# Out projection of a hybrid decoder layer: its sums kept in PSUM over all row blocks, parts of x made pair by pair, weight ring of the second gate in another place

## The chip, the cores and the metric

One Trainium2 chip, one of its cores. Five engines work side by side, each on its own list of instructions in order: TensorE (PE) multiplies into PSUM, VectorE (DVE) and ScalarE (ACT) work elementwise and can read PSUM, GpSimd (POOL) works elementwise on SBUF, and SyncE (SP) issues most of the DMAs. The metric is the device time of one launch in microseconds (us), lower is better. It is the median of several runs.

## The reference

One decoder layer on x of 1024 tokens by 1024 columns, float32: SwiGLU with 2816 hidden rows, layer norm, a token mixer of two branches, layer norm, a second SwiGLU, layer norm.

```python
def swiglu(x, w_gate, w_up, w_down):
    return (jax.nn.silu(x @ w_gate) * (x @ w_up)) @ w_down

# in token_mixer
    y_a = hm @ w_branch_a
...
    y_b = yr @ w_branch_b
    merged = jax.nn.sigmoid(gate_a) * y_a + jax.nn.sigmoid(gate_b) * y_b
    return merged @ w_out

# in reference
        x = layer_norm(ALPHA * x + 0.5 * swiglu(x, ffn1_w_gate[l], ffn1_w_up[l], ffn1_w_down[l]),
                       ln1_g[l], ln1_b[l])
        mix = token_mixer(x, w_in[l], m_conv_w[l], ...
        x = layer_norm(ALPHA * x + mix, ln2_g[l], ln2_b[l])
        x = layer_norm(ALPHA * x + 0.5 * swiglu(x, ffn2_w_gate[l], ffn2_w_up[l], ffn2_w_down[l]),
                       ln3_g[l], ln3_b[l])
```

## The kernel before

**Every product is three matmuls.** A float32 operand is split into a high part (`nc.scalar.copy` to a rounded type, on ACT) and a low part (the difference, on POOL or DVE); `mm3` adds high by high, high by low and low by high into one PSUM bank. `split` (L126) makes the two parts, L130 is the high one, L134 the low one.

**The stages in order.** Gate and up projection of the first SwiGLU (`gate_first`, `gate_rest`), its down projection (`down_all`), the token mixer (`middle`, phases B and C), phase D (rest of branch a, out projection, second layer norm, parts of x for the second gate), gate and up projection of the second SwiGLU (`gate_rest`), its down projection (`down_all`), the last layer norm.

**The gate** works on 7 combinations of blocks of x and of the weights instead of 8 blocks. For each pair of token tiles `put_sums` makes the 7 sums and differences of x on DVE, transposes each on PE (`put`, L212), and writes the high part (ACT, L215) and the low part (DVE, L216). For each of the 22 hidden blocks f, `weights` makes the 7 sums of the weights (DVE, L254) and their splits (ACT and POOL, 7 of each), into the ring `wr` of 14 buffers, which holds one f; `gate_up` runs 7 products of 12 matmuls in the banks g, b and c, with the additions between them (L275, L299, L303 on DVE; L287, L291, L298 on ACT), and stores h in eight DMAs of 64 KB. The first f is done in two halves of 256 columns: half A needs the token pairs 0 and 1 only. The stores of the last f are issued by ACT, all others by SP. In the first gate the ring lies in a pool of its own on the left side of the memory, in the second in the pool R2 on the right side, with the raw weights `rw` and the sums `tw`, and the second down projection goes on using it.

**The down projection** (`down_all`) goes through the tokens in groups of 3, 3 and 2 tiles. A group holds up to 6 PSUM banks over all 22 rows of weights; each row is loaded and split again for each group. At the end the banks are added to the residual (L379) and the layer norm of each tile is run inside the next group.

**Phase D** does what is left of branch a (10 of its 16 products of 24 matmuls; the other 6 run in phase C and go to memory), and the out projection of 384 matmuls. It takes the rows of w_out two at a time, and for each token tile adds the product of two rows to the residual y in SBUF (`down`, L404), which makes 64 such additions. The layer norm of a tile follows its last addition (L415 to L429), and when all 8 tiles are done, `put_sums` runs for the four pairs.

**What sets the order.** A scheduler puts the instructions of each engine in an order; buffers are rings, and whoever writes one waits for its last reader. All loads of SP stand in one queue.

Of the kernel before, what the change touches and what calls it, by code (L numbers as in the profile page):

```python
# [8 lines left out]
F32 = mybir.dt.float32  # L9
# [21 lines left out]
class Net:  # L31
# [16 lines left out]
    RING = {"rw": (8, F32), "tw": (6, F32), "wr": (14, F32R), "e": (14, F32)}  # L48
# [11 lines left out]
    def ring(self, tag, n=512):  # L60

        bufs, dt = self.RING[tag]
        return {"e": self.ep, "wr": self.wp}.get(tag, self.rp).tile([P, 512], dt, tag=tag, bufs=bufs, name=self.nm(tag))[:, :n]
# [154 lines left out]
    def put_sums(self, cmb, p, a1, a2, s1):  # L218

        tt_ = self.nc.vector.tensor_tensor  # L220
        self.put(cmb[0], p, a1[0], "a")
        tt_(s1, a2[0], a2[1], op=ALU.add)
        tt_(a2[0], a1[0], a2[0], op=ALU.subtract)
        self.put(cmb[1], p, a1[1], "c")
        tt_(a1[0], s1, a1[0], op=ALU.subtract)
        self.put(cmb[2], p, a1[0], "d")
        self.put(cmb[3], p, a2[0], "c")
        tt_(a1[1], a1[1], a1[0], op=ALU.subtract)
        self.put(cmb[4], p, s1, "a")
        self.put(cmb[5], p, a2[1], "c")  # L230
        self.put(cmb[6], p, a1[1], "d")
# [38 lines left out]
    def gate_up(self, cmb, f, ws, hD, c0=0, c1=512):  # L270
# [35 lines left out]
    def gate_first(self, pre, src, cmb, hD):  # L306

        nc = self.nc
        B = []

        def pair(p):
            a = [[self.ring("e") for _ in range(2)] for _ in range(2)]
# [5 lines left out]
            self.put_sums(cmb, p, *a, self.ring("tw"))  # L318

        pair(0)  # L320
# [6 lines left out]
        self.gate_rest(pre, cmb, hD, 1)  # L327

    def gate_rest(self, pre, cmb, hD, f0):
        for f in range(f0, NF):  # L330
            ws = self.weights(*(self.raws(pre, f, 0) + self.raws(pre, f, 1)))
            if f == 0:
                self.gate_up(cmb, f, ws, hD, 0, 256)
                self.gate_up(cmb, f, ws, hD, 256, 512)
            else:
                self.gate_up(cmb, f, ws, hD)

    def down_all(self, pre, src, hD, ln_cb, hook=None):

        nc = self.nc  # L340
        wd = self.I[f"{pre}_w_down"][0]
        y, late = [], []
# [3 lines left out]
        for tag, shape, bufs in (("lng", [P, D], 1), ("hr", [P, 384], 4), ("lnb", [P, D], 1)):  # L346
            self.s(tag, shape, bufs=bufs)
        for t0, n in ((0, 3), (3, 3), (6, 2)):
            acc = [[self.ps(tag) for _ in range(2)] for tag in "gbc"[:n]]
            for f in range(NF):  # L350
                hr = self.s("hr", [P, 384], bufs=4)[:, :n * P]
# [1005 lines left out]
```

## Time and profile before

| what | us |
|---|---|
| median of 3 runs | 3258.95 (3255.22 to 3263.72) |
| profiled execution | 3261.03 |
| span of the profiled execution | 3259.1 |
| first gate | 0 to 470 |
| first down projection | 475 to 720 |
| phases B and C | 720 to 2332 |
| phase D, up to the second gate's first matmul | 2332 to 2555 |
| second gate | 2555 to 2995 |
| second down projection and last layer norm | 3000 to 3259 |

The profile lists for each instruction when it began, how long it took and what released it. Instructions of one engine overlap a little, so that durations add up to more than busy time. A busy share is an average over stages with different limits; what matters is where PE stands still, and for whom.

### The profile page before, as it was taken

How to read it: one execution, taken by the hardware profiler on the slowest of the kernel's cores; microseconds unless marked ns; L12 is line 12 of the kernel's file. 1: busy time of each engine (PE TensorE's matmuls, PEld its weight loads, DVE VectorE, ACT ScalarE, POOL GpSimd, SP SyncE). 2: the span in 40 equal slices, each digit the busy share in tenths (PEclk: the TensorE clock that was granted, in tenths of full speed). 3: DMA queues.
4: the chain of work that ended last, by engine and by line, in shares of the span. 5: the costliest groups of instructions: out<-in, count | busy, mean ns of one | idle time of the engine just before them, and what ended most of it. 6: DMA issues, size and time to landing. Idle time of an engine off the chain costs nothing. (4 is left out here: it accounts for less than half of the span.)

```text
span 3259.1 us, 45659 instructions
## 1 busy us (share of the span) xinstructions
PE 3084.5 (95%) x15888; PEld 2500.5 (77%) x15888; DVE 1928.2 (59%) x4820; ACT 1085.7 (33%) x1796; POOL 757.2 (23%) x819
## 2 busy tenths in 40 slices
PE   6999999999899999999999999999998799999997
PEld 6888878877677777887877777777776688887886
DVE  6444434683657676757577766476559744443557
ACT  3333324453312232323222222376332333332444
POOL 3444420011212222222222122200000344442000
PEclk8999999999889999999999999999999899999999
DMA  4223236662222222222232323474562322223665
GB/s 120 81 81 88 85 94 225 201 218 71 64 52 76 71 76 65 74 69 69 63 74 67 78 80 88 145 240 146 175 211 86 101 84 82 83 78 116 206 206 183
DMA packets 492908, 364.37 MB, mean 112 GB/s; under 512 B 114141, under 2 KB 415879, under 8 KB 492679
## 3 DMA queue, kind: packets, MB, share of 16 engines
q1 hardware_dynamic: 483463, 347.84, 36.2%
q0 software_dynamic: 4608, 8.39, 1.0%
q10 hardware_dynamic: 4608, 5.24, 0.5%
q8 instruction: 125, 2.05, 0.3%
q14 instruction: 104, 0.85, 0.1%
HBM read 280.61 MB, written 80.74 MB: 111 GB/s over the span
## 5 line engine op out<-in xcount | busy, mean ns | idle before, releaser
L150 PE MATMUL psg<-xT,wf 128*128 128x512 f32 x2328 | 632.1, 407 | 0.7 <-ACT f L860 0.7
L150 PEld LDWEIGHTS psg<-xT,wf 128*128 128x128 f32 x2328 | 422.3, 190 | 75.6 <-ACT f L860 1.1
L130 ACT CAST wr<-rw 128x512 fp32r<-128x512 f32 x396 | 243.9, 621 | 454.6 <-PE psc L150 243.0
L150 PE MATMUL psa<-xT,w 128*128 128x512 f32 x1200 | 317.9, 407 | 8.0 <-DVE pj L496 5.0
L134 POOL TENSOR_TENSOR wr<-tw,wr 128x512 fp32r<-128x512 f32 x176 | 229.2, 1304 | 264.2 <-ACT wr L130 258.3
L134 DVE TENSOR_TENSOR wr<-rw,wr 128x512 fp32r<-128x512 f32 x264 | 182.9, 699 | 178.7 <-ACT wr L130 167.6
L134 POOL TENSOR_TENSOR wr<-rw,wr 128x512 fp32r<-128x512 f32 x132 | 173.7, 1316 | 493.9 <-ACT wr L130 493.8
L150 PEld LDWEIGHTS psa<-xT,w 128*128 128x128 f32 x1200 | 223.5, 192 | 59.9 <-DVE pj L496 9.8
L275 DVE TENSOR_TENSOR e<-psb,e 128x512 f32<-128x512 f32 (+1 forms) x138 | 92.2, 668 | 296.6 <-PE psb L150 296.6
L150 PE MATMUL psb<-xq,wr 128*128 128x512 f32 (+1 forms) x1104 | 260.7, 386 | 6.5 <-DVE e L275 4.8
L150 PE MATMUL psc<-xq,wr 128*128 128x512 f32 (+1 forms) x1104 | 259.1, 384 | 1.5 <-DVE e L275 1.5
L150 PEld LDWEIGHTS psb<-xq,wr 128*128 128x128 f32 x1104 | 204.7, 192 | 48.5 <-issue 3.0
L150 PEld LDWEIGHTS psc<-xq,wr 128*128 128x128 f32 x1104 | 202.8, 190 | 43.5 <-DVE e L275 1.7
L150 PE MATMUL psg<-wr,wr 128*128 128x512 f32 x792 | 211.8, 397 | 16.4 <-ACT wr L130 11.4
L130 ACT CAST wr<-tw 128x512 fp32r<-128x512 f32 x176 | 109.0, 621 | 313.3 <-PE psb L150 226.6
L150 PE MATMUL psb<-wr,wr 128*128 128x512 f32 x792 | 209.1, 394 | 0.0
L150 PEld LDWEIGHTS psg<-wr,wr 128*128 128x128 f32 x792 | 149.1, 190 | 53.4 <-ACT wr L130 12.7
L134 POOL TENSOR_TENSOR w<-raw,w 128x512 fp32r<-128x512 f32 (+1 forms) x51 | 65.3, 1294 | 491.9 <-ACT w L130 430.6
L150 PEld LDWEIGHTS psb<-wr,wr 128*128 128x128 f32 x792 | 150.4, 190 | 31.7
L134 POOL TENSOR_TENSOR wf<-rawf,wf 128x512 fp32r<-128x512 f32 x98 | 129.7, 1339 | 166.9 <-ACT wf L130 151.6
L774 POOL TENSOR_SCALAR S<-S,PC 128x128 f32<-128x128 f32 x120 | 80.2, 668 | 292.6 <-DVE S L776 181.4
L150 PE MATMUL psc<-wr,wr 128*128 128x512 f32 x528 | 134.2, 389 | 0.0
(365 smaller groups left out, 5352.3 us busy)
## 6 DMA issues: line engine op xcount, KB each, us to landing
rw<-in_ffn_w_down_dram SPq DMA_DIRECT2D x264, 256.0 KB
rawf<-in_w_in_dram SPq DMA_DIRECT2D x98, 256.0 KB
rw<-in_ffn_w_gate_dram SPq DMA_DIRECT2D x88, 256.0 KB
rw<-in_ffn_w_up_dram SPq DMA_DIRECT2D x88, 256.0 KB
h<-e SPq DMA_DIRECT2D x336, 64.0 KB
hr<-h SPq DMA_DIRECT2D x88, 192.0 KB
raw<-in_w_in_dram SPq DMA_DIRECT2D x50, 256.0 KB
qkD<-f SPq DMA_DIRECT2D x32, 256.0 KB
```

Of the source, the lines that this page charges most:

```text
L130: nc.scalar.copy(hi, src)
L134: eng.tensor_tensor(lo, src, hi.bitcast(F32), op=ALU.subtract)
L150: self.nc.tensor.matmul(out, a[u], b[v], start=first and i == 0, stop=last and i == 2, skip_group_check=more)
L275: add = lambda o, a, b: nc.vector.tensor_tensor(o, a[:, cs], b, op=ALU.add)
L774: nc.gpsimd.tensor_scalar(S1, S, pcn, None, op0=ALU.mult)
```

## The change

- `gate_first` loads x of the pairs 0 to 2 before any sum is made, then makes pair 0's sums, loads pair 3, makes pair 1's sums, half A, the sums of the pairs 2 and 3, half B.
- `gate_up` stores h in two DMAs of 256 KB for each f. `gate_rest` loads the first two rows of the following down projection ahead of its last block (`row_load`, `ahead`), into a ring `hr` of the pools R1 and R2.
- All 16 products of branch a go to memory (`mix`, `mgD` is now 1024 by 1024). The out projection is `down_all` with w_out as its weights and 8 rows. Its layer norm calls `put_sums` when a pair of tiles is done: pair 0's in group 2, pair 1's in group 3, the others behind it. w_out is now loaded and split three times, not twice.
- The ring `wr` of the second gate lies in a pool W2 of its own on the right side, below R2 and E2; the second down projection has its own ring.
- `put_sums` takes a list of banks; `held` has the meaning that `loaded` had.

```diff
+    def row_load(self, wd, hD, t0, n, f):
+
+        hr, raws = self.ring("hr", n * P), [self.ring("rw") for _ in range(2)]
+        self.nc.sync.dma_start(hr, hD[f * P:(f + 1) * P, t0 * P:(t0 + n) * P])
+        for c in range(2):
+            self.loaded = self.nc.sync.dma_start(raws[c], wd[f * P:(f + 1) * P, c * 512:(c + 1) * 512])
+        return hr, raws
...
         def store(e, t):
-            for p in range(c0 // P, c1 // P):
-                dma(hv[:, e, p], t[:, p * P - c0:(p + 1) * P - c0])
+            dma(hv[:, e, c0 // P:c1 // P], t.rearrange("r (p t) -> r p t", t=P))
...
+        pair = lambda p: self.put_sums(cmb, p, *A[p], self.ring("tw"))
+        for p in range(4):
+            if p == 3:
+                pair(0)
+            A.append([[self.ring("e") for _ in range(2)] for _ in range(2)])
             for e in range(2):
                 for c in range(2):
-                    nc.sync.dma_start(a[e][c], src[(2 * p + e) * P:(2 * p + e + 1) * P, c * 512:(c + 1) * 512])
+                    nc.sync.dma_start(A[p][e][c], src[(2 * p + e) * P:(2 * p + e + 1) * P, c * 512:(c + 1) * 512])
             if p < 2:
                 B.extend(self.raws(pre, 0, p))
...
             ws = self.weights(*(self.raws(pre, f, 0) + self.raws(pre, f, 1)))
+            if f == NF - 1:
+                ahead = [self.row_load(wd, hD, 0, 3, i) for i in range(2)]
...
-    def down_all(self, pre, src, hD, ln_cb, hook=None):
+    def down_all(self, wd, nf, src, hD, ln_cb, hook=None, ahead=()):
...
-                if f % 3 == 2 and late:
+                if (f % 3 == 2 if nf == NF else f % 2) and late:
                     late.pop(0)()
...
+    def mix(self, xT, js, halves=(0,)):
+
+        its = [self.branch_a(j, lambda sl, g, j=j: self.nc.sync.dma_start(self.mgD[j * P:(j + 1) * P, sl], g)) for j in js]
+        alts = ["", "f"] if len(js) == 2 else ["f" if js[0] % 2 else ""]
+        self.proj_many(xT, its, self.I["w_branch_a"][0], alts, halves=halves, ps="g", lo_eng="dve")
...
+        def done2(tt, y):
+            nc.sync.dma_start(x2D[row(tt), :], y[tt])
+            if tt % 2:
+                net.put_sums(cmb, tt // 2, *([t[:, c] for c in c2] for t in y[tt - 1:tt + 1]), net.ring("tw"), "ad")
...
+            with net.phase("O", UB=5, side="right"):
+                net.wp = net.sp
+                net.down_all(ins["w_out"][0], NK, x1D, net.mgD, fin2, lambda: gb2.extend(rows("ln2")))
+            with net.pool("E2", "right") as net.ep, net.pool("W2", "right") as net.wp:
+                ahead = net.gate_rest("ffn2", cmb, h2, 0)
...
+    with net.phase("D", VB=6):
+        net.mix(hmT, (6, 7))
+        for j in range(0, NK, 2):
+            net.mix(hmT, (j, j + 1), (1,))
```

SP's queue at the start of the program, before: the loads of x for pair 2 (`e_374` on) stand behind the weights of f=1 (`rw_606` to `rw_612`), of f=2 and the first stores of h.

```order
L241 DMA rw_762<-in_ffn_w_gate_dram 128x4x128
L241 DMA rw_764<-in_ffn_w_up_dram 128x4x128
L241 DMA rw_766<-in_ffn_w_gate_dram 128x4x128
L241 DMA rw_768<-in_ffn_w_up_dram 128x4x128
L284 DMA h_77<-e_270 128x128 x2
L315 DMA e_374<-in_x_dram 128x512
L284 DMA h_77<-e_272 128x128 x2
L315 DMA e_375<-in_x_dram 128x512
```

And now; `e_122` to `e_125` are pair 2, `e_184` to `e_187` pair 3, `rw_602` on the weights of f=1.

```order
L318 DMA e_122<-in_x_dram 128x512
L318 DMA e_123<-in_x_dram 128x512
L318 DMA e_124<-in_x_dram 128x512
L318 DMA e_125<-in_x_dram 128x512
L318 DMA e_184<-in_x_dram 128x512
L318 DMA e_185<-in_x_dram 128x512
L318 DMA e_186<-in_x_dram 128x512
L318 DMA e_187<-in_x_dram 128x512
L243 DMA rw_602<-in_ffn_w_gate_dram 128x4x128
```

The loads of x have moved ahead of the weights of f=1 and of every store.

PE's queue where phase C ends, before: `psg_20608` is a product of phase C, `psb_21497` the first one of phase D's half 1, `psg_21287` another of phase C.

```order
L150 MATMUL psg_20608<-xT_19892,wf_20598 128x512
L150 MATMUL psg_20608<-xT_19891,wf_20599 128x512
L150 MATMUL psg_20608<-xT_19891,wf_20598 128x512
L150 MATMUL psb_21497<-xT_21320,w_21477 128x512
L150 MATMUL psg_21287<-xT_19891,wf_21277 128x512
```

And now, in the same place: `psg_20475` is what `psg_20608` was, `psg_21154` what `psg_21287` was.

```order
L151 MATMUL psg_20475<-xT_19759,wf_20465 128x512
L151 MATMUL psg_20475<-xT_19758,wf_20466 128x512
L151 MATMUL psg_20475<-xT_19758,wf_20465 128x512
L151 MATMUL psg_20475<-xT_19759,wf_20465 128x512
L151 MATMUL psg_21154<-xT_19758,wf_21144 128x512
```

The matmul with `w_21477` no longer stands between the two.

DVE's queue in the out projection, before: additions to y, splits of rows of w_out (`u`), the first layer norm.

```order
L404 SCALAR_TENSOR_TENSOR y_21357<-y_21357,psc_21777 128x512
L404 SCALAR_TENSOR_TENSOR y_21358<-y_21358,psc_21785 128x512
L404 SCALAR_TENSOR_TENSOR y_21358<-y_21358,psc_21793 128x512
L1124 TENSOR_TENSOR v_22418<-psg_22393,v_22418 128x512
L134 TENSOR_TENSOR u_21804<-u_21801,u_21803 128x1024
L134 TENSOR_TENSOR u_21810<-u_21807,u_21809 128x1024
L404 SCALAR_TENSOR_TENSOR y_21355<-y_21355,psc_21817 128x512
L404 SCALAR_TENSOR_TENSOR y_21355<-y_21355,psc_21825 128x512
L415 BN_STATS lnst_21834<-y_21355 128x6 x2
```

And now, in group 2: L135 are splits of rows for the matmuls, L217 and L225 to L230 belong to the sums of pair 0, L404 is now a layer norm's multiplication.

```order
L217 TENSOR_TENSOR xT_21648<-psd_22145,xT_21647 128x4x128
L135 TENSOR_TENSOR wr_22264<-rw_22251,wr_22263 128x512
L404 TENSOR_TENSOR u_21834<-u_21834,lng_21754 128x1024
L225 TENSOR_TENSOR u_21832<-u_21830,u_21832 128x512
L135 TENSOR_TENSOR wr_22301<-hr_22294,wr_22300 128x384
L227 TENSOR_TENSOR u_21830<-tw_22135,u_21830 128x512
L135 TENSOR_TENSOR wr_22305<-rw_22295,wr_22304 128x512
L230 TENSOR_TENSOR u_21830<-u_21830 128x512
L217 TENSOR_TENSOR xT_21650<-psd_22160,xT_21649 128x4x128
```

The 64 additions are gone from this queue; layer norm and sums of x now stand between the splits that feed PE.

## Rows read from the trace of the kernel before

**Rows 1.** The page's first part: busy time of each engine, its share of the span, instructions.

```profile
PE 3084.5 (95%) x15888; PEld 2500.5 (77%) x15888; DVE 1928.2 (59%) x4820; ACT 1085.7 (33%) x1796; POOL 757.2 (23%) x819
```

**Rows 2.** Windows: the stretch in us and its length, then busy time (and instructions) of PE, of PE's weight loads, of DVE, ACT and POOL, then the granted clock as a share, the DMA share and GB/s.

```profile
20.00:40.00 20.00, 12.66 (x80) 11.71 (x78) 9.02 (x16) 6.83 (x12) 7.93 (x6) 0.83 0.28 78
40.00:60.00 20.00, 14.46 (x84) 12.49 (x85) 14.60 (x22) 8.22 (x15) 1.63 (x1) 0.74 0.35 107
480.00:720.00 240.00, 238.11 (x1059) 195.37 (x1059) 150.71 (x282) 113.45 (x206) 3.91 (x3) 0.99 0.68 219
2455.00:2555.00 100.00, 73.98 (x316) 55.26 (x316) 92.94 (x181) 35.06 (x50) 0.00 (x0) 0.85 0.32 107
```

**Rows 3.** Timeline of PE at the start: start, duration, engine, line, operation, tiles, shape, count, and in brackets the idle time before it and what ended it.

```profile
34.91 1.60 PE L150 MATMUL psc<-xq,wr 128*128 128x256 f32 x12
40.47 0.81 PE L212 MATMUL psa<-ident,e 128*128 128x128 f32 x4 [3.96 <-DMA e<-in_x_dram]
...
72.96 2.21 PE L150 MATMUL psb<-xq,wr 128*128 128x512 f32 x9
```

**Rows 4.** Timeline of SP's queue at the start: a load of pair 2 and the seven behind it.

```profile
37.38 0.38 SPq L315 DMA_DIRECT2D e<-in_x_dram  x1
...
38.81 3.32 SPq L315 DMA_DIRECT2D e<-in_x_dram  x7
```

**Rows 5.** Timeline of DVE at the start: a subtraction beside POOL, two writes of x back to back, the last write of x.

```profile
55.14 1.76 DVE L254 TENSOR_TENSOR tw<-rw,rw 128x512 f32<-128x512 f32 x1
...
57.43 0.68 DVE L216 TENSOR_TENSOR xq<-psa,xq 128x512 fp32r<-128x512 f32 x1
58.03 0.68 DVE L216 TENSOR_TENSOR xq<-psc,xq 128x512 fp32r<-128x512 f32 x1
...
61.63 0.69 DVE L216 TENSOR_TENSOR xq<-psd,xq 128x512 fp32r<-128x512 f32 x1
```

**Rows 6.** Timeline of all engines between the first gate and its down projection.

```profile
469.69 4.11 ACTq L284 DMA_DIRECT2D h<-e  x8
...
471.02 0.69 DVE L303 SCALAR_TENSOR_TENSOR e<-e,e 128x512 f32<-128x512 f32 x1
...
474.31 0.51 ACT L130 CAST wr<-hr 128x384 fp32r<-128x384 f32 x1 [5.38 <-DMA hr<-h]
...
475.39 3.23 PE L150 MATMUL psg<-wr,wr 128*128 128x512 f32 x6 [5.13 <-ACT wr L130]
```

**Rows 7.** The same place of the second SwiGLU, PE alone.

```profile
2999.69 3.23 PE L150 MATMUL psg<-wr,wr 128*128 128x512 f32 x6 [5.07 <-ACT wr L130]
```

**Rows 8.** Timeline of PE where phase C ends.

```profile
2332.60 0.84 PE L150 MATMUL psg<-xT,wf 128*128 128x512 f32 x3
2336.95 0.50 PE L150 MATMUL psb<-xT,w 128*128 128x512 f32 x1 [3.51 <-ACT w L130]
2337.29 7.26 PE L150 MATMUL psg<-xT,wf 128*128 128x512 f32 x24
```

**Rows 9.** Timeline of PE: the last matmuls of the out projection, the first of the second gate, and the first of its second block f.

```profile
2513.50 5.89 PE L150 MATMUL psc<-u,u 128*128 128x512 f32 x24
...
2555.20 5.47 PE L150 MATMUL psg<-xT,wr 128*128 128x256 f32 x24 [1.19 <-ACT wr L130]
...
2584.55 2.94 PE L150 MATMUL psg<-xT,wr 128*128 128x512 f32 x12
```

**Rows 10.** Groups of DVE's instructions from 2455 to 2555 us, by shape: count, busy time, mean ns of one, idle time before them. The first and the last of 25 rows, and some between.

```profile
L404 DVE SCALAR_TENSOR_TENSOR y<-y,psc 128x512 f32<-128x512 f32 x36 | 24.3, 677 | 4.4 <-PE psc L150 4.0
L429 DVE SCALAR_TENSOR_TENSOR y<-y,lnr,lnb 128x1024 f32<-128x1024 f32 x8 | 9.9, 1277 | 0.0
...
L420 DVE TENSOR_TENSOR y<-y,lng 128x1024 f32<-128x1024 f32 x7 | 8.5, 1215 | 0.0
L415 DVE BATCH_NORM_STATS2 lnst<-y 128x6 f32<-128x512 f32 x12 | 8.0, 683 | 0.0
...
L164 DVE SCALAR_TENSOR_TENSOR lnr<-rst,lnr 128x2 f32<-128x2 f32 x12 | 1.8, 149 | 0.1
...
L425 DVE TENSOR_SCALAR lnv<-lnmv 128x2 f32<-128x2 f32 x4 | 0.6, 158 | 0.0
```

**Rows 11.** Groups of DVE's instructions in the first down projection, 480 to 720 us: the splits.

```profile
L134 DVE TENSOR_TENSOR wr<-rw,wr 128x512 fp32r<-128x512 f32 x123 | 84.1, 689 | 85.8 <-ACT wr L130 78.8 <-PE psc L150 5.4 <-issue 0.3
L134 DVE TENSOR_TENSOR wr<-hr,wr 128x384 fp32r<-128x384 f32 x41 | 22.6, 551 | 0.0
```

**Rows 12.** Windows of 100 us in the first gate and in the second, columns as in Rows 2.

```profile
200.00:300.00 100.00, 100.00 (x443) 82.81 (x442) 43.49 (x61) 31.68 (x53) 47.24 (x38) 1.00 0.28 79
...
2700.00:2800.00 100.00, 100.00 (x432) 81.07 (x431) 41.96 (x58) 30.84 (x52) 46.19 (x37) 1.00 0.28 80
```

**Rows 13.** Timeline of PE in the first gate and in the second, each with two groups of 12 matmuls that follow each other.

```profile
249.77 2.88 PE L150 MATMUL psb<-xq,wr 128*128 128x512 f32 x12
252.49 2.88 PE L150 MATMUL psc<-xq,wr 128*128 128x512 f32 x12
...
2930.32 2.96 PE L150 MATMUL psb<-xq,wr 128*128 128x512 f32 x12
2933.11 2.95 PE L150 MATMUL psc<-xq,wr 128*128 128x512 f32 x12
```

More of the change, by code (lines that the diff above doesn't have):

```diff
@@ L336, in gate_rest @@
                 self.gate_up(cmb, f, ws, hD)
[L338 removed]
+        return ahead
+    def row_load(self, wd, hD, t0, n, f):
[5 more added lines that the diff above has]
+    def down_all(self, wd, nf, src, hD, ln_cb, hook=None, ahead=()):
         nc = self.nc
[L341 to L342 removed]
+        y, late, ahead = [], [], list(ahead)
         if self.wp is self.sp:
             self.ring("wr")
[L346 to L347 removed]
         for t0, n in ((0, 3), (3, 3), (6, 2)):
             acc = [[self.ps(tag) for _ in range(2)] for tag in "gbc"[:n]]
[L350 to L352 removed]
+            for f in range(nf):
+                hr, raws = ahead.pop(0) if ahead else self.row_load(wd, hD, t0, n, f)
+                if (t0, f) == (6, 17):
+                    self.held = self.loaded
                 h = self.ring("wr", n * P), self.ring("wr", n * P)
@@ L1226, in build @@
                 net.wp = net.sp
-                net.down_all("ffn1", x, h1, fin1, hook1)
+                net.down_all(ins["ffn1_w_down"][0], NF, x, h1, fin1, hook1, ahead)
         middle(net, ins, x1T, x1D)
-        y, gb2 = [], []
-        def load_ln():
-            gb2.extend((net.bcast_row(ins["ln2_g"], "lng"), net.bcast_row(ins["ln2_b"], "lnb")))
-        def load_y(hh):
-            for tt in range(4 * hh, 4 * hh + 4):
-                nc.sync.dma_start(y[tt], x1D[row(tt), :])
-        def fin2(tt):
-            net.layer_norm(tt, y, *gb2, lambda t: nc.sync.dma_start(x2D[row(t), :], y[t]))
@@ L1243, in build, with rows @@
-        c2 = slice(0, 512), slice(512, 1024)
-        with net.phase("D", UB=10, VB=5, side="right"):
-            load_ln()
-            v = [net.half() for _ in range(5)]
-            yt = [net.s("y", [P, D], bufs=8) for _ in range(8)]
-            y.extend(yt[4:] + yt[:4])
-            net.mix_out(net.hmT, y, fin2, load_y)
-            a, b = net.new_xT(), net.new_xT()
-            gw.close()
+        gw.close()
+        gb2, gb3 = [], []
+        c2 = slice(0, 512), slice(512, 1024)
+        def rows(v):
+            return net.bcast_row(ins[v + "_g"], "lng"), net.bcast_row(ins[v + "_b"], "lnb")
@@ L1252, in build, with fin2 @@
+        def fin2(tt, y):
+            net.layer_norm(tt, y, *gb2, lambda t: done2(t, y))
+        def done2(tt, y):
+            nc.sync.dma_start(x2D[row(tt), :], y[tt])
+            if tt % 2:
+                net.put_sums(cmb, tt // 2, *([t[:, c] for c in c2] for t in y[tt - 1:tt + 1]), net.ring("tw"), "ad")
+        with net.rings("R2"):
             xp = xs.enter_context(net.pool("X2"))
-            (a11, a12), (s2, s3), (s1, a22) = net.halves(a), net.halves(b), net.halves([net.big(xp) for _ in range(2)])
+            (a11, a12), (s2, s3) = (net.halves(net.new_xT()) for _ in range(2))
+            s1, a22 = net.halves([net.big(xp) for _ in range(2)])
@@ L1254, in build @@
             d = net.big(xp)
             cmb = [a11, a12, s2, s3, s1, a22, (d[:, 0:4], d[:, 4:8])]
-            for p in range(4):
-                net.put_sums(cmb, p, *([y[2 * p + e][:, c] for c in c2] for e in range(2)), net.half())
-        with net.rings("R2"):
-            net.wp = net.rp
-            with net.pool("E2", "right") as net.ep:
-                net.gate_rest("ffn2", cmb, h2, 0)
+            with net.phase("O", UB=5, side="right"):
+                net.wp = net.sp
+                net.down_all(ins["w_out"][0], NK, x1D, net.mgD, fin2, lambda: gb2.extend(rows("ln2")))
@@ L1273, in middle @@
     with net.phase("B", VB=4):
-        with tc.issue_after(net.loaded.ins):
+        with tc.issue_after(net.held.ins):
             net.rwkv_small(x1T)
@@ L1311, in middle @@
             net.mlstm_chunk(c)
-        hmT = net.hmT = [net.new_xT()]
+        hmT = [net.new_xT()]
         with net.low():
```

113 lines of the change are left out of this document (27 added, 86 removed).

## The prediction, made before the changed kernel ran

> **What bounds the kernel now.** I read the page first: PE is busy for 95% of the span, DVE for 59% [rows 1]. So a gain must come from places where PE stands still, or from a stage where its matmuls follow each other more slowly than elsewhere. The windows find the places: 20 to 60 us has PE at 27.1 of 40 us with a clock of 0.74 to 0.83, and 2455 to 2555 has it at 74.0 of 100, while DVE there is busy for 92.9 [rows 2]. The timeline adds two stops of 5.1 us, between each gate and its down projection [rows 6, 7]. Elsewhere there is little to take: in the first down projection PE works 238.1 of 240 us [rows 2]. The windows of the two gates show the slower stage: 443 matmuls in 100 us in the first, 432 in the second, both at a clock of 1.00 and with the other engines alike [rows 12].
>
> In phases B and C the instructions of PE stand in the same order as before, so I count nothing there.
>
> **The start.** Half A ends at 34.91 + 1.60 = 36.5 us. Then PE waits 4.0 us for x [rows 3], because the loads of pairs 2 and 3 are issued from 37.38 to 42.1 us, behind weights and stores [rows 4]. The last part of x is written by DVE at 61.63 [rows 5], and the next f's matmuls run evenly from 72.96 on [rows 3], 11.3 us later. Now x is there early. What is left behind half A is 13 writes of x and 4 other steps of DVE; back to back one takes 0.60 us (57.43 to 58.03 [rows 5]), so 17 x 0.60 = 10.2, with 1.0 for the first transposition and cast. Ten subtractions move into half A, beside POOL's work; such a one took 1.76 us instead of 0.69 [rows 5], and half A's own additions stand behind them in DVE's queue. That is 10 x 1.07 = 10.7 us at most, nothing if they fit in DVE's idle time there (11 of 20 us, [rows 2]); I take 3, as POOL's seven splits cover only a part of half A. So: 36.5 + 3 + 11.2 + 11.3 = 62.0 instead of 73.0, **-11 us**. Bounds: -14 with no delay; -4 with the whole of it.
>
> **Gate to down projection, twice.** ACT issues the eight stores of the last f in 4.11 us, 0.51 each, and the casts for the first matmul stand behind them: the cast at 474.31, the matmul at 475.39 [rows 6]. Now there are two issues; the second one waits for DVE's last step, which ends at 471.71 [rows 6]. 471.7 + 0.5 + 1.1 (cast to matmul, as now) = 473.3, **-2.1** each, -4.2 together. The rows of weights were not what it waited for, so their earlier loads count nothing. Bounds: 0 to -5 each, as the slow first matmuls behind a stop (six take 3.23 us [rows 6], where 6 x 0.227 = 1.4) may go too. A page of the Trainium skill speaks against this term: "DMA: Bandwidth & Descriptors", in its section on the fixed cost, puts a sequencer's dispatch of a DMA at about 50 ns. By it eight issues are 0.4 us and this term would be -0.3; the row has 4.11, so I keep the row's.
>
> **End of phase C and branch a.** PE stops for 3.51 us at 2333 for a matmul of phase D whose weights were cast late, and the 24 matmuls behind it, which could have run, take 7.26 us instead of 24 x 0.227 = 5.4 [rows 8, 13]. That matmul has left its place, so both go. From 2332.6 on 284 matmuls are left of branch a: 284 x 0.227 = 64.4, with 2 us for four places where PE now waits until DVE has read its bank (each at most the 0.69 us of that step, less the matmuls that stand between; 5.4 in all if the old stop stays in some form): 2399. Then a new wait: the first cast of the out projection stands behind the last addition of branch a, as it overwrites its buffers: two steps of 0.69 and two casts of 0.5 to 0.6, with their hand-overs 2.8 us: 2401.8. The transfers of this stretch, 1.28 MB for each 24 matmuls or 5.44 us, make 235 GB/s; in the first down projection 219 GB/s went beside PE at 238.1 of 240 us [rows 2], so I count them as hidden.
>
> **Out projection.** The same 384 matmuls. Group 1 holds 8 rows of 18: 144 x 0.227 = 32.6, with 1.5 for the first splits: 2435.9. From there DVE decides, and its work is counted from rows [rows 10, 11]: 15 rows of splits (0.551 + 2 x 0.689) = 28.9; 16 additions out of PSUM at 0.68 = 10.9; 8 layer norms (2 x 0.683, 1.215, 1.277 and two small steps, 4.2) = 33.6; 4 inverse roots (11 steps of 0.15) = 6.6; 28 writes of x and 16 sums at 0.683 = 30.1; 6 sums of weights at 0.69 = 4.1. Together 114. Durations overlap: in the window from 2455 to 2555 the 25 rows add up to 105 us and DVE is busy for 92.9 [rows 2, 10], so 114 x 0.885 = 101. It stood idle for 7.1 of those 100 us; now two group ends wait for PE, so I take 10, and 1 to the first matmul: 2435.9 + 101 + 10 + 1 = 2548, before 2555.2 [rows 9]. **-7**. What cost 64 additions now costs 16, but a third of the splits is new, and all the layer norms and sums remain on DVE; that is why the gain is small. The stretch from the gate's first matmul to its even pace (29.4 us, to 2584.55) I leave as it is: PE gets the last transpositions first, as before. Bounds: -15 with DVE never idle and both stops at 2333 and 2399 gone; +10 if DVE stands idle for 27 instead of 10 us.
>
> **The second gate's pace.** 12 matmuls take 2.79 us there and 2.72 in the first gate [rows 13]; the seven products of a block f make 0.49 us, 22 blocks (less the first, in halves) 21 x 0.49 = 10.3. The order of work is the same in both gates; what differs is where the operands lie: in the first gate the ring of the weights lies below x, in the second at the upper end of the memory, far above x. The down projections have both operands in one ring, the first at 0.225 a matmul (238.1 over 1059 [rows 2], smaller ones among them), so it is only this combination that is slow. The ring now lies next to x's parts, below the rings it was above. No row shows this new place; the bounds are 0 and -10.3, and I take **-10.3**, since all stretches but that one run at 0.227. A rule of the Trainium skill says the opposite: "SBUF — State Buffer", section "Who interferes with whom", gives PE read ports of its own and lets only the port that DVE and GpSimd share contend. By it the place of a ring changes nothing and this term is 0, which is the first rival; the row of 2.79 it doesn't explain.
>
> **Sum.** -11 - 4.2 - 7 - 10.3 = -32.5 against the profiled execution's own time, 3261.03 (span 3259.1 and 1.9 around it): 3228.5. That execution is 2.1 above the median of 3258.95; against the median it is 3226.5. I say 3228.
>
> **The rivals.**
> 1. *The pace stays.* The second gate goes on at 2.79, whatever the reason for it is. Against it: nothing but the place differs. For it: no row shows the new place. -22: 3239.
> 2. *The out projection gives nothing, and the pace stays.* DVE, busy for 93% of the window now, stays the bound; each idle piece that the new order brings costs in full, and the time saved at 2333 goes into it. With D at 0 and the start at -6: -10, 3250, the same.
> 3. *Slower: DVE and PE wait for each other in the groups 2 and 3.* The writes of x for pairs 0 and 1 (14 of them) now stand in DVE's queue between the splits, and their transpositions in PE's queue behind matmuls that need such splits. Before, no matmuls stood ahead of them there. If each write waits for a whole row of PE (18 or 12 matmuls, 4.1 or 2.7 us, 3.4 in the middle), that is 14 x 3.4 = 48 us: 3228.5 + 48 = 3276. It decides for slower from 3.0 us for each write on (14 x 3.0 = 42, the 32.5 gained and 9.8). Against it: the ring holds two rows ahead, and the first down projection runs layer norms with transpositions between its splits while PE works 238.1 of 240 us [rows 2].
> 4. *The change doesn't reach the start:* x is early, but half A gets longer by as much, since POOL and DVE slow each other. Start 0, rest as forecast: 3239.
>
> **How the numbers follow.** Forecast 0.42; rivals 1 and 4 together 0.27; rival 2 0.17; rival 3 0.08; still more gain (no idle time on DVE, half A not delayed, both down projections at -5, about 3212) 0.06. About 0.3% (9.8 us) is what a measurement of this kernel can tell from no change. Faster: 0.42 + 0.27 + 0.06 = 0.75, of which I give 0.02 to the same; the same 0.17 + 0.02 = 0.19; slower 0.08. The range leaves out rival 3 and most of the far gain: from 3213 to 3256, the upper end 3 us short of the old median for rival 2 with the start at its worst.
>
> **What would show it.** Start: no wait for x at 40 us, and even groups of 12 matmuls from about 62 us on. Gates' ends: stops of 3.1 us instead of 5.1. Phase C's end: no stop for weights at 2333 (the times shifted by the start's gain). Out projection: DVE above 90% from the end of group 1 to the second gate, waits of PE for splits in group 3; PE waiting in pieces of 3 us or more in group 2 means rival 3. Second gate: 443 matmuls in 100 us, or 432 for rival 1. The forecast is wrong as a whole if phases B and C, which nothing touches, come out longer by themselves.

## The result, and the profile after

The changed kernel took 3242.07 us (median of 4 runs, 3237.07 to 3244.4), the one before on the same chip 3259.64: a ratio of 0.993, with a 95% interval of 0.9911 to 0.9949. On another chip it was 3240.21 beside 3266.22, 0.9917 (0.9899 to 0.9934). So the change saves 18 to 26 us, clear of no change but less than the 31 forecast: 3228 was forecast, with a range of 3213 to 3256.

The page's first part after: DVE has 20 us less to do than in [rows 1], PE 7, and the span is 18.8 shorter.

```profile
PE 3077.5 (95%) x15888; PEld 2496.7 (77%) x15888; DVE 1908.0 (59%) x4812; ACT 1097.3 (34%) x1836; POOL 757.8 (23%) x819
```

**Start.** Windows, columns as in [rows 2]:

```profile
20.00:40.00 20.00, 15.04 (x105) 13.68 (x105) 17.60 (x26) 8.39 (x16) 9.61 (x6) 0.91 0.29 81
40.00:60.00 20.00, 18.01 (x136) 16.16 (x135) 16.14 (x25) 10.63 (x20) 8.74 (x6) 1.00 0.22 64
```

PE's timeline after, with the place where [rows 3] had a wait of 3.96 us for x:

```profile
35.47 1.67 PE L151 MATMUL psb<-xq,wr 128*128 128x256 f32 x12 [1.73 <-DVE e L277]
37.19 1.66 PE L151 MATMUL psc<-xq,wr 128*128 128x256 f32 x12
38.69 0.60 PE L213 MATMUL psc<-ident,e 128*128 128x128 f32 x4
...
60.55 2.88 PE L151 MATMUL psb<-xq,wr 128*128 128x512 f32 x12
```

Half A ends at 38.85 (37.19, with 1.66), 2.3 us later than the 36.5 of before, since DVE has the first pairs' subtractions ahead of its additions. In exchange the parts of x follow at once, and the even pace begins at 60.55 instead of 72.96.

**First gate to first down projection.** All engines, to be held against [rows 6]:

```profile
457.26 2.57 ACTq L285 DMA_DIRECT2D h<-e  x2
...
458.59 0.69 DVE L304 SCALAR_TENSOR_TENSOR e<-e,e 128x512 f32<-128x512 f32 x1
459.88 0.51 ACT L131 CAST wr<-hr 128x384 fp32r<-128x384 f32 x1 [3.37 <-DVE e L304]
...
460.96 3.23 PE L151 MATMUL psg<-wr,wr 128*128 128x512 f32 x6 [3.13 <-ACT wr L131]
```

The stop is 3.13 us instead of 5.13. The cast now begins 0.05 us after ACT has issued the two stores (457.26 + 2.57 = 459.83). Before, it began 0.5 us after the end of the eight issues, and what released it was the load of the first row of h [rows 6], which the change has moved ahead as well. The six slow matmuls behind the stop are unchanged.

**End of phase C to the second gate.** PE's timeline of the mix (what is left of branch a's products) and the first matmul of the out projection (before: [rows 8, 9]):

```profile
2341.46 5.70 PE L151 MATMUL psg<-xT,wf 128*128 128x512 f32 x24 [0.88 <-DVE h L1108]
2350.89 7.32 PE L151 MATMUL psg<-xT,w 128*128 128x512 f32 x24 [3.73 <-DVE v L1108]
...
2398.91 0.55 PE L151 MATMUL psg<-wr,wr 128*128 128x512 f32 x1 [2.63 <-ACT wr L131]
```

The stop of 3.51 us at 2333 is gone. In its place stands one of 3.73, with slow matmuls behind it (24 in 7.32). The wait before the out projection, 2.63, is the one foreseen (2.8). Then windows of group 2, of group 3, and of the pairs' end up to the gate's first matmul:

```profile
2434.00:2473.00 39.00, 39.00 (x187) 32.22 (x186) 37.77 (x75) 20.98 (x37) 0.00 (x0) 1.00 0.61 198
2473.00:2502.00 29.00, 24.21 (x110) 16.87 (x108) 28.77 (x71) 14.49 (x26) 0.00 (x0) 1.00 0.60 191
2502.00:2535.00 33.00, 13.90 (x57) 9.80 (x57) 29.03 (x54) 11.02 (x18) 0.07 (x1) 0.55 0.19 72
```

DVE is busy for 95.6 of 101 us, above the 90% that the forecast named; PE works all through group 2 and stands idle for 19 us of the last 33.

**The second gate's pace** is still 432 in 100 us, as in [rows 12] (PE alone: instructions, clock, DMA share, GB/s):

```profile
2600.00:2700.00 100.00, 100.00 (x432) 1.00 0.29 83
```

**Second gate to second down projection.** Where [rows 7] had one stop of 5.07, there are now two:

```profile
2971.14 2.63 ACTq L285 DMA_DIRECT2D h<-e  x2
...
2974.95 0.50 PE L151 MATMUL psg<-wr,wr 128*128 128x512 f32 x1 [3.19 <-ACT wr L131]
...
2979.05 0.56 DVE L135 TENSOR_TENSOR wr<-hr,wr 128x384 fp32r<-128x384 f32 x1 [5.83 <-DMA h<-e]
...
2980.26 2.50 PE L151 MATMUL psg<-wr,wr 128*128 128x512 f32 x5 [4.81 <-DVE wr L135]
```

The first is the short one that was forecast. The second is new: DVE's split waits 5.83 us for the last stores of h, although it reads nothing of them. It writes a buffer of the new ring, and that lies where the last store reads its e tile: in the program as built the buffer begins at byte 167360 of a partition, the e tile at 167872, and each is 2048 long.

Set side by side, the same matmuls of two executions give a ledger: how much each stretch adds to the time after against before, in us (minus is a gain). The second pair of profiles is from the repeats told below.

| term | forecast | first pair | second pair |
|---|---|---|---|
| start, to the first gate's even pace | -11 | -12.4 | -13.9 |
| first gate to first down | -2.1 | -1.8 | -3.0 |
| phases A to C | 0 | +6.2 | -2.3 |
| end of C to the second gate's even pace | -7 | -14.8 | -16.5 |
| the second gate's pace | -10.3 | 0.0 | 0.0 |
| second gate to the end | -2.1 | +4.0 | +3.1 |
| span | -32.5 | -18.8 | -32.6 |

Three rows differ from the forecast by more than 5 us in both pairs, and one only in the first.

### The profile page after: what moved, and what is told of

Same layout as the page of the kernel before. It is cut to its first block, busy times and chain, and to the rows that moved or that the text cites. A ratio compares the mean times of both kernels' runs of the same rounds, so it can differ in the third digit from the quotient of the medians.

```text
span 3240.3 us, 45588 instructions
## 1 busy us (share of the span) xinstructions
PE 3077.5 (95%) x15888; PEld 2496.7 (77%) x15888; DVE 1908.0 (59%) x4812; ACT 1097.3 (34%) x1836; POOL 757.8 (23%) x819
## 5 line engine op out<-in xcount | busy, mean ns | idle before, releaser
L151 PE MATMUL psg<-xT,wf 128*128 128x512 f32 x2352 | 640.6, 409 | 1.6 <-DVE h L1108 0.9
L151 PEld LDWEIGHTS psg<-xT,wf 128*128 128x128 f32 x2352 | 429.0, 191 | 78.2 <-ACT wf L131 1.3
L131 ACT CAST wr<-rw 128x512 fp32r<-128x512 f32 x444 | 273.2, 621 | 490.5 <-PE psc L151 276.7
L135 DVE TENSOR_TENSOR wr<-rw,wr 128x512 fp32r<-128x512 f32 x312 | 215.5, 697 | 197.2 <-ACT wr L131 186.5
L135 POOL TENSOR_TENSOR wr<-tw,wr 128x512 fp32r<-128x512 f32 x176 | 229.9, 1308 | 248.9 <-ACT wr L131 234.9
L135 POOL TENSOR_TENSOR wr<-rw,wr 128x512 fp32r<-128x512 f32 x132 | 173.4, 1314 | 481.9 <-ACT wr L131 481.7
L151 PE MATMUL psg<-wr,wr 128*128 128x512 f32 x936 | 253.4, 398 | 23.5 <-DVE wr L135 13.3
L151 PE MATMUL psb<-wr,wr 128*128 128x512 f32 x936 | 250.5, 395 | 0.0
L151 PEld LDWEIGHTS psg<-wr,wr 128*128 128x128 f32 x936 | 175.8, 190 | 69.0 <-DVE wr L135 20.7
L151 PEld LDWEIGHTS psb<-wr,wr 128*128 128x128 f32 x936 | 178.1, 191 | 37.3
L135 POOL TENSOR_TENSOR w<-raw,w 128x512 fp32r<-128x512 f32 (+1 forms) x51 | 65.5, 1297 | 491.5 <-ACT w L131 429.9
L135 POOL TENSOR_TENSOR wf<-rawf,wf 128x512 fp32r<-128x512 f32 x98 | 130.0, 1342 | 169.6 <-ACT wf L131 154.0
L151 PE MATMUL psc<-wr,wr 128*128 128x512 f32 x624 | 160.1, 391 | 0.0
```

Source lines behind the costliest of these rows:

```text
L131: nc.scalar.copy(hi, src)
L135: eng.tensor_tensor(lo, src, hi.bitcast(F32), op=ALU.subtract)
L151: self.nc.tensor.matmul(out, a[u], b[v], start=first and i == 0, stop=last and i == 2, skip_group_check=more)
```

## Experiments

Each kernel is the changed one with the edit shown. Where an expectation says "12.4 us earlier" or the like, it is a row of this ledger. The medians of one kernel differ by some us from measurement to measurement (the kernel before 3259.64 to 3266.22, the changed one 3242.07 and 3240.21), so what an edit of 10 us is worth is read from the same matmuls in its trace and in the changed kernel's.

**128 bytes between the second gate's pools**

```diff
-            with net.pool("E2", "right") as net.ep, net.pool("W2", "right") as net.wp:
+            with net.pool("E2", "right") as net.ep, net.pool("pad2", "right") as pp, net.pool("W2", "right") as net.wp:
+                pp.tile([P, 32], F32, tag="pad2", bufs=1, name="pad2")
```

> The changed kernel with 128 more bytes between the second gate's pools, so that its weight ring begins at 137024 bytes of a partition instead of 137152; nothing else moves. Theory A (the address): a matmul goes at 227 ns when its weights and its columns begin at the same offset of 256 bytes, and at 232 when the two offsets differ by 128, as they do in the second gate before and after the change (weights at 192 of 256, x at 64) and in no other place. Then the second gate goes at 2.72 us per 12 matmuls, PE is busy with 443 instead of 432 instructions in 100 us, and the time falls by 10.3 us, to about 3232. Rival B (the place: which end of the partition the ring lies at, or what else runs then): the pace stays at 2.79 and the time at 3242, within 3.

3232.52 us. The gate runs at 443:

```profile
2700.00:2800.00 100.00, 100.00 (x443) 1.00 0.29 83
```

From its even pace to its end the same matmuls gain 10.0 us on the changed kernel. The place of the ring is that of the changed kernel but for 128 bytes, so the place is not the reason: theory A holds. (An offset is meant here as the address in a partition, modulo 256 bytes.)

**The mirror: 128 bytes in the first gate**

```diff
-            with net.pool("W1") as net.wp, net.pool("X1") as xp, net.pool("E1", "right") as net.ep:
+            with net.pool("W1") as net.wp, net.pool("pad1") as pp, net.pool("X1") as xp, net.pool("E1", "right") as net.ep:
+                pp.tile([P, 32], F32, tag="pad1", bufs=1, name="pad1")
```

> The changed kernel with 128 bytes put between the first gate's weight ring and its x, so that x there begins at 192 of 256 and the weights still at 64; the ring stays where it was. Theory A (offsets that differ by 128 cost 5.8 ns a matmul): the first gate, 21 row blocks of 84 matmuls, falls from 443 to 432 instructions in 100 us and the time grows by 10.2 us, to about 3252. Rival B (the place of the ring or what else runs decides): the first gate keeps 443 and the time stays at 3242, within 3.

3252.1 us, 10.0 above the changed kernel's 3242.07, and 9.9 more in the first gate by the same matmuls, which goes at the second's pace:

```profile
200.00:300.00 100.00, 100.00 (x432) 1.00 0.30 85
```

A ring below x, fast until now, becomes slow by 128 bytes. Both directions are shown. The pads leave one rival, that each operand has to begin at 64 of 256, whatever the other does. The second down projection of the changed kernel speaks against it: weights and columns lie in one ring there, both at 192 in the program as built, and they go at the fast pace.

```profile
3060.00:3160.00 100.00, 100.00 (x443) 1.00 0.60 194
```

**64 bytes in the second gate.** The edit of the first experiment with a tile of [P, 16].

> The changed kernel with 64 more bytes between the second gate's pools: the weight ring begins at 128 of 256 bytes, x at 64. Theory A (128 bytes' difference alone costs, through which of two halves of 256 bytes an operand begins in): 64 and 128 lie in different halves, so the pace stays at 2.79 us per 12 matmuls and the time at 3242. Theory B (any difference of the offsets costs): the same. Theory C (only a difference of just 128 costs, 64 doesn't): 443 instructions in 100 us and -10.3 us, about 3232. So a fast pace leaves C alone, a slow one A or B.

The pace stays slow, so theory C falls:

```profile
2600.00:2700.00 100.00, 100.00 (x430) 1.00 0.30 87
```

The time was 3236.03, 4 below that of the changed kernel beside it; no row at this place explains that. Whether any difference costs or only one across halves, and whether the offset counts modulo 256 or 512, stays open.

**The gate's ring kept for the second down projection**

```diff
-            with net.pool("E2", "right") as net.ep, net.pool("W2", "right") as net.wp:
-                ahead = net.gate_rest("ffn2", cmb, h2, 0)
+            with net.pool("W2", "right") as net.wp:
+                with net.pool("E2", "right") as net.ep:
+                    ahead = net.gate_rest("ffn2", cmb, h2, 0)
...
-                net.wp = net.sp
```

> The changed kernel with the second gate's weight ring kept open for the second down, which then has no ring of its own in the place that the gate's e tiles held. Theory: the 4.8 us wait for VectorE at the second down's first matmuls is the ring's buffers waiting for the last two stores of h, which read e tiles in that place; with another ring VectorE's split doesn't wait, the stop of 3.2 us at the first matmul stays near 3.1, as in the first down, and the time falls by 4.5 to 6, to about 3237. Rival: VectorE or the loads are late there anyway, the wait stays under another name, and the time stays at 3242, within 2.

3231.97 us, and 11.4 us gained at this place: twice what was expected, since the first stop and the slow matmuls went too. All engines there:

```profile
2964.61 0.51 ACT L131 CAST wr<-hr 128x384 fp32r<-128x384 f32 x1 [1.68 <-PE psb L151]
...
2970.17 2.94 PE L151 MATMUL psc<-xq,wr 128*128 128x512 f32 x12
...
2972.95 1.53 PE L151 MATMUL psg<-wr,wr 128*128 128x512 f32 x6
```

The first row is cast 8 us before the gate's last matmul ends, and PE goes from gate to down projection without a pause. So the stop is not only the issues on ACT, to which the forecast had put it down, but also the change of pools: a new pool's buffers wait for the last readers of what lay there, while a ring's come free one by one. A kept ring alone doesn't do it, though. In the kernel before, the second down projection went on using the gate's ring too, and PE stopped for 5.07 us [rows 7]; there the rows of h were loaded only at 2995.58, after ACT had begun the last stores (2993.99), and the first cast waited:

```profile
2995.58 1.86 SPq L352 DMA_DIRECT2D hr<-h  x4
2998.61 0.51 ACT L130 CAST wr<-hr 128x384 fp32r<-128x384 f32 x1 [5.38 <-DMA h<-e]
```

The changed kernel loads the first two rows ahead but has a new ring, and stops for 3.19 and 4.81. Only with both does the stop go.

**The mix's stores on GpSimd's queue**

```diff
-        its = [self.branch_a(j, lambda sl, g, j=j: self.nc.sync.dma_start(self.mgD[j * P:(j + 1) * P, sl], g)) for j in js]
+        dma = (self.nc.gpsimd if halves[0] or js[0] == 6 else self.nc.sync).dma_start
+        its = [self.branch_a(j, lambda sl, g, j=j: dma(self.mgD[j * P:(j + 1) * P, sl], g)) for j in js]
```

> The changed kernel with the ten stores of the merged rows in the last part of the mix sent from GpSimd's queue instead of SyncE's. Theory: the 3.7 us wait near 2351 and the twelve or so matmuls at half clock behind it (about 1.9 us) come from a load that stood behind such a store in SyncE's queue; with the stores away the mix ends 4 to 6 us sooner and the time falls by as much, to about 3237. Rival: the load is late for its own reason, or what the mix gains the out projection waits for (its first loads of merged rows stand behind the stores still), and the time stays at 3242, within 2.

3240.27 us, the wait 2.5 instead of 3.7; but the repeat of the changed kernel has 2.4 there with no edit, and the run with 128 bytes in the second gate 3.9, so the edit has not shown an effect. It missed its store: the one ahead of the load is that of row 5, still issued in phase C, which stayed with SyncE. SyncE's queue in this kernel:

```profile
2342.28 1.31 SPq L1131 DMA_DIRECT2D mgD<-h  x1
2343.64 0.42 SPq L1106 DMA_DIRECT2D v<-gD  x1
```

That this store makes the wait is argued from the queue's order and not shown.

**Low parts of w_out's rows on GpSimd**

```diff
-                    self.split(raws[c], *d, lo_eng="dve")
+                    self.split(raws[c], *d, lo_eng="pool" if nf == NK else "dve")
```

> The changed kernel with the low parts of w_out's rows in the out projection made on GpSimd instead of VectorE (48 splits of 128x512, 16 of them in each group of token tiles). Theory: groups 2 and 3 and the pairs behind them are bound by VectorE, which is busy for 95.6 of the 101.3 us from the end of group 1 to the gate's first matmul; without 32 of its splits of about 0.65 us there (21 us) the stretch falls to about 85 with TensorE's share of clock as it is, and the time falls by 10 to 18, to about 3228. Rival: GpSimd takes longer for a split than VectorE has time between rows, or slows VectorE beside it, so that rows come no sooner, and the time is 3242 or above.

3253.64 us, 0.9963 of the kernel before (0.9947 to 0.9978) where the changed kernel has 0.993: about 11 us more. Groups of DVE from group 2 to the gate, of the changed kernel first (count, then busy time and mean ns of one):

```profile
L135 DVE TENSOR_TENSOR wr<-rw,wr 128x512 fp32r<-128x512 f32 x30 | 20.3, 680 | 1.0 <-PE psc L151 1.0
L399 DVE BATCH_NORM_STATS2 lnst<-u 128x6 f32<-128x512 f32 x16 | 10.9, 681 | 0.0
...
L404 DVE TENSOR_TENSOR u<-u,lng 128x1024 f32<-128x1024 f32 x8 | 9.7, 1215 | 0.0
...
L135 DVE TENSOR_TENSOR wr<-hr,wr 128x256 fp32r<-128x256 f32 x8 | 3.2, 399 | 0.0
```

And with GpSimd at work, DVE and then GpSimd:

```profile
L404 DVE TENSOR_TENSOR u<-u,lng 128x1024 f32<-128x1024 f32 x8 | 11.9, 1486 | 0.0
...
L399 DVE BATCH_NORM_STATS2 lnst<-u 128x6 f32<-128x512 f32 x16 | 10.3, 669 | 0.0
L135 DVE TENSOR_TENSOR wr<-hr,wr 128x256 fp32r<-128x256 f32 x8 | 6.1, 760 | 3.2 <-ACT wr L131 3.2
```

```profile
L135 POOL TENSOR_TENSOR wr<-rw,wr 128x512 fp32r<-128x512 f32 x31 | 48.1, 1569 | 67.3 <-ACT wr L131 65.1 <-DMA rw<-in_w_out_dram 1.5 <-DMA hr<-mgD 0.7
```

The rival holds: GpSimd takes 1569 ns for what DVE does in 680, and DVE's steps beside it grow, from 1215 to 1486 and from 399 to 760. So this doesn't test whether DVE's load sets the stretch; the next experiment does, in part.

**One ring from the out projection through the second gate**

```diff
+            with net.pool("W2", "right") as net.wp:
                 with net.phase("O", UB=5, side="right"):
-                    net.wp = net.sp
                     net.down_all(ins["w_out"][0], NK, x1D, net.mgD, fin2, lambda: gb2.extend(rows("ln2")))
-            with net.pool("E2", "right") as net.ep, net.pool("W2", "right") as net.wp:
+                with net.pool("E2", "right") as net.ep:
                     ahead = net.gate_rest("ffn2", cmb, h2, 0)
```

> The changed kernel with one weight ring from the out projection through the second gate; the second down has its own, as in the changed kernel. In the run with all rings kept this part stood 4.6 us earlier at the out projection's first matmul and 10.3 us more at the second gate's even pace, since the gate's first weights needn't wait until the out projection's pool is free and its matmuls go between the last pairs' transposes. Theory: -13 to -16 here, about 3228, with the stop and the wait at the second gate's end as in the changed kernel. Rival: that gain came from the first ring or the offset in that run, or from their combination: -5 or less, 3237 or above.

3226.93 us, 13.3 less than the changed kernel beside it. PE's timeline:

```profile
2492.48 1.67 PE L151 MATMUL psg<-xT,wr 128*128 128x256 f32 x12 [0.17 <-DVE rst L164]
...
2514.19 3.29 PE L151 MATMUL psg<-xT,wr 128*128 128x256 f32 x12
...
2546.68 2.96 PE L151 MATMUL psb<-xT,wr 128*128 128x512 f32 x12
...
2961.76 3.24 PE L151 MATMUL psg<-wr,wr 128*128 128x512 f32 x6 [6.12 <-ACT wr L131]
```

The gate's first matmuls fill the gaps between the last pairs. In the changed kernel they couldn't: they stood behind the out projection's pool. DVE's work is the same, so for its last part the stretch was bound not by DVE alone but by what PE was allowed to do meanwhile. The stop at the second down projection is still there, 6.12.

**All rings kept, offsets equal.** The edits of both ring experiments together, the first gate's ring kept for the first down projection in the same way, and

```diff
-    ctx.enter_context(net.pool("pad", "right")).tile([P, 8], F32, tag="pad", bufs=1, name="pad")
+    ctx.enter_context(net.pool("pad", "right")).tile([P, 40], F32, tag="pad", bufs=1, name="pad")
```

> The changed kernel with one weight ring kept open from the first gate through the first down, and one from the out projection through the second gate and the second down, and with the rings 128 bytes lower, so that weights and x of both gates begin at the same offset of 256 bytes. If the gains of the single edits add up: -10.3 for the offset, -11.4 at the second gate's end, at the first gate's end the 3.1 us stop and the slow matmuls behind it (about 6.5), so about 3214. Rival: each of these only shows the next wait (a load of h's last rows, VectorE's splits), and less than 22 us come of it: 3220 or above.

3198.13 us, a ratio of 0.9797 (0.9773 to 0.9821) to the kernel before, below the changed kernel's 0.993 too. Theory and rival both fell short of the gain: besides the single gains expected, the out projection's 13 us are in it, which that sum had left out. The first gate's border, which no run has alone, shows 6.5 us in this one's trace: its matmuls stand 2.2 us later than the changed kernel's before the border and 4.4 earlier behind it.

**The old start, twice**

```diff
-        for p in range(4):
-            if p == 3:
-                pair(0)
-            A.append([[self.ring("e") for _ in range(2)] for _ in range(2)])
...
+        def pair(p):
+            a = [[self.ring("e") for _ in range(2)] for _ in range(2)]
...
+        pair(0)
         pair(1)
```

> The changed kernel with the first gate's start as before the change (x loaded pair by pair as the buffers come free, pair 0 summed before pair 1's loads are issued). Theory: the 12.4 us that the same matmuls stand earlier from the first gate on come from the four pairs' loads that are issued at once, and nothing later gives them back; the first gate's even pace begins 12 us later and the time grows by 11 to 13, to about 3254. Rival: what is saved at the start is waited for later (by loads that are then late in B or C, which came out 5.8 us longer), and the time grows by 6 or less, to 3248 at most.

3246.35 us (7 runs) beside a before of 3264.08. In the profile the first gate's end is 13.8 us later than in the changed kernel, but the middle then shorter, so that 1.7 is left. That spoke for the rival, so it was run again beside the changed kernel:

> The old start once more, beside the changed kernel on the same chip. Its first run was 13.8 us later than the changed kernel after the first gate and only 1.7 later at the end of the mLSTM chunks, at a higher granted clock in between. Theory A (the throttle's chance in that profile): the median is 9 to 13 us above the changed kernel's of this call. Theory B (a later start is given back in the middle): it is 6 us or less above, and the profile shows again a stretch from the first down to the end of the chunks that is 8 us or more shorter than the changed kernel's.

3248.41 us (8 runs, 3241.73 to 3262.49), 8.2 above the changed kernel beside it: between the two theories. Its profile's span, 3247.2, is 12.7 above that of the changed kernel there, 3234.4, and its middle is as long as others. So A is nearer, and the first profile had a short middle by chance; how much of the 12 us is kept on average, 8 or all, isn't settled.

**Before and after once more**

> The kernel before once more, for a second profile of it. The stretch from the first down to the end of the mLSTM chunks took 5.8 us more in the changed kernel's profile than in the one of before, with the same instructions in the same order; in the profiles of four kernels that differ from the changed one elsewhere, it came out 2.1 less to 1.9 more than in the changed one. Theory A (the change makes the stretch longer through what it moved in memory): this profile has it as short as the first, within 2 us. Theory B (the first profile of before caught a short one): it comes out 3 us or more longer than the first.

> The changed kernel once more, to stand beside the old start on the same chip and for a second profile. If the 5.8 us that its first profile had more than the first of before in the stretch from the first down to the end of the mLSTM chunks are the throttle's (a second profile of before had 5.6 us more than its first there, at a lower granted clock), its stretch lies between those two again and its time is 0.993 of before, within 0.003. If the change makes the stretch longer, it is 5 us or more above the second profile of before.

The stretch from the first down projection to the end of the chunks, by the same two matmuls, in four kernels: before, its repeat, after, its repeat (columns as in [rows 2]):

```profile
494.71:2297.68 1802.97, 1720.58 (x9850) 1385.51 (x9849) 1177.26 (x3650) 596.09 (x977) 351.23 (x492) 0.97 0.37 104
```

```profile
495.52:2304.05 1808.53, 1724.24 (x9849) 1387.45 (x9848) 1176.54 (x3650) 595.56 (x977) 351.26 (x492) 0.97 0.37 104
```

```profile
480.53:2289.64 1809.11, 1726.36 (x9849) 1390.00 (x9848) 1177.78 (x3650) 596.30 (x977) 351.42 (x492) 0.97 0.37 104
```

```profile
478.57:2284.84 1806.27, 1718.83 (x9850) 1382.28 (x9849) 1177.28 (x3650) 595.57 (x977) 351.26 (x492) 0.97 0.37 104
```

1803.0 and 1808.5 before, 1809.1 and 1806.3 after; all other runs lie between 1797.0 (the first old start) and 1813.2 (all rings). DVE's work is equal within 1.3 us. The two of before differ most within one short piece, and there by the granted clock, 1.00 and 0.98 (PE alone):

```profile
1963.11:2140.21 177.10, 170.17 (x1001) 1.00 0.46 139
```

```profile
1964.16:2144.14 179.98, 172.68 (x1000) 0.98 0.45 136
```

Theory B holds: the 5.8 us are not the change's.

## Why the prediction was right, and where it was not

**Start: right.** -11 forecast, -12.4 and -13.9 measured at the first gate's even pace. No wait for x, and even groups from 60.55 on, where about 62 was forecast; the delay of half A, taken as 3, was 2.3. In the whole time the old start cost 8.2, so that all of it is kept to the end isn't shown.

**First gate to first down projection: right,** -1.8 and -3.0 of -2.1. The cause named (two issues for eight) fits the rows, but the first rows of h and of the weights are now also loaded earlier (the prediction counted the weights' as nothing and h's not at all), and no run has one without the other: before, the load of a row of h was what released the cast. The Trainium skill's dispatch of 50 ns ("DMA: Bandwidth & Descriptors", section "Anatomy of one DMA — SWDGE (gpsimd) path") would have given -0.3. That section is on the path of GpSimd's DMAs, and these stores are ACT's; the trace, with 0.51 for each issue before, goes with the row.

**Second gate to second down projection: wrong.** The step that failed is "-2.1 each". The stop itself shrank as forecast, from 5.07 to 3.19. But the change moved the second gate's ring, and with it what the second down projection's ring overlays: the e tiles of the last f, whose stores were under way. A second stop of 4.81 and slow matmuls came of it, +4.0 in all. The order shows no such wait; the addresses would have. With the ring kept and the rows loaded ahead, 11.4 us more were to be had at this place.

**The second gate's pace: wrong.** -10.3 was taken because only "this combination" of places was slow, and rival 1 was given a part of 0.27, together with rival 4. The pace stayed, as rival 1 has it. Place was the wrong reading of the rows: in the programs as built, weights and x begin at the same offset of 256 bytes in the first gate (64 and 64) and at different ones in the second (192 and 64), before and after alike. 128 bytes put this right in the one gate (10 us less) and wrong in the other (10 us more). So the size of the term was right and would have been had for a pad. The rule of the Trainium skill quoted in the prediction ("SBUF — State Buffer", "Who interferes with whom") gave 0 for the move, which is what came; but by its table the columns and the weight loads of PE have independent read ports, and nothing there would make the offset between the two cost 2%. The runs show that it does, and the measurement decides; why, they don't show.

**End of C to the second gate: right in sign, too small,** -14.8 and -16.5 for -7. Several sizes were off in the first pair. From the old stop's place to the mix's end 71.7 us were needed (2324.57 to 2396.28) instead of 66.4, for the new stop of 3.73 and its slow matmuls: +5.3. Group 1 took 34.7 for 34.1, the wait before it 2.6 for 2.8. From group 1's end to the gate 101.3 instead of 112: DVE busy for 95.6 and idle for 5, where 101 and 10 were taken; a split of 256 columns takes 0.399, and the sum had 0.551 for each row. And from the gate's first matmul to its even pace 26.8 instead of the unchanged 29.4. Rival 3 (PE waiting for each write in group 2) didn't happen: PE is busy for 39.0 of 39.0 us there.

**Phases A to C: right at 0,** although the first pair showed +6.2. The prediction had named this as what would prove it wrong as a whole; the repeat showed the same 5.6 us between two executions of the kernel before. The mean of the two pairs, -25.7, is the forecast with each term's error put in: -32.5 + 10.3 (pace) + 5.7 (second down projection) - 8.7 (out projection) - 2.2 (start) + 2.0 (the middle) - 0.3 (first down projection) = -25.7. Most of the miss of the first result, 14 us, is the pace; the other errors nearly cancel. So the time fell inside the range in part by luck: the pace term failed altogether and rival 1 (3239) was nearer, and that the second pair's span gained 32.6, just the forecast, is luck too, since the 15.5 us missing from the pace and the second down projection came from places forecast smaller.

## What to carry to other kernels

A new pool at the border of two stages makes the first splits of the next stage wait for the last readers of the old tiles. With one ring across the border (and, into the down projections, the first rows loaded ahead), three such borders were worth 6, 13 and 11 us here, together more than the 12 to 14 us of the loads at the start and the 2 to 3 of the issues (the 6 shows only within the run with all rings). Where one stage's matmuls are evenly slower than another's, compare the offsets of weights and columns before their places; a pad of 128 bytes was worth 10 us. And price a change by the same matmuls in both traces, place by place: the middle moved by 7 us between two executions of one kernel (the old start) and by 16 over all runs, nearly the whole gain of the first measurement.

## What was not expected of the hardware

A matmul of 128x512 goes at 226 ns where weights and columns begin at the same offset of 256 bytes (both at 64, or both at 192: 443 in 100 us) and at 232 where the offsets differ by 64 or by 128 (430 to 432), at a granted clock of 1.00 in both. The runs don't show the reason.

GpSimd slows only some of DVE's steps. With its splits beside them, those that read two tiles of SBUF grew on average (1215 to 1486 ns, 399 to 760; single ones took 2.30 us, others no longer than alone), and the statistics, which read one, did not (681 and 669). The Trainium skill says so in "SBUF — State Buffer", "Who interferes with whom": an instruction of DVE with two inputs from SBUF contends with GpSimd's reads, one with at most one doesn't, outside DVE's two-port modes. In these rows the trace agrees.
